# TensorE operands placed modulo 128 bytes in SBUF, and kv weights in rows of 256 columns

## The chip, the cores and the metric

The kernel runs on one core of one Trainium2 chip. The metric is the device time of one execution in microseconds (us). A core has a matrix engine (TensorE, shown as PE, with its weight loads shown apart as PEld), VectorE (DVE), ScalarE (ACT), GpSimd (POOL) and SyncE (SP), which issues most DMA transfers. Operands of TensorE lie in SBUF, products land in PSUM.

A product on TensorE takes two operands from SBUF. The *stationary* operand (the weights, here always up to 128 columns) is brought in by a weight load; the *moving* operand, of 64 to 512 columns here, is then streamed past it. While one moving operand is streamed, the weight load of the next product is already under way, so two reads of SBUF run side by side. This text calls the *place* of an operand the byte address of its first column within a partition, modulo 128. All columns are 4 bytes.

## The reference

One layer of an encoder is computed for 1024 prompt rows and 64 sample rows of width 1024 (with 512 cached rows behind the sample). Cut to what matters:

```python
z = x @ w_in                       # q, k, v of two kinds of attention, u and v of a gate
o = concat(fox_attention, u * (W_s v + b), stick_breaking_attention)
x = layer_norm(ALPHA * x + rms(o) * g_mix @ w_out)
x = layer_norm(ALPHA * x + relu(x @ w_up) ** 2 @ w_down)     # 1024 -> 4096 -> 1024
```

All products are exact to about float32: each operand is split into a high part and a rest, and three products (high by high, high by rest, rest by high: `PASSES`) are summed. The two products of the MLP are done with seven block products instead of eight (a scheme of Strassen's kind).

## The kernel before

The work runs in four stages, by the times at which TensorE does them.

- *Projections and attention, 0 to 542 us.* `tok_mm` (L476, matmuls at L485) makes k and v of a pair of heads, and the gate's u and v: the stationary operand is a block of 128 rows of x (`xT`, 128 columns), the moving one is 256 columns of a weight tile `wkv` (262 columns for the first pair, which takes the forget gate's 6 columns along). `wkv` holds, for each of 8 blocks of rows, the high part and the rest, each in a row of 262 columns, of which all pairs but the first use 256. `q_stage` (L616, L626) makes q with the weights (`wq`) stationary and 256, 320 or 384 columns of `xT` moving. `qk_rows` (L684), `Unit.b_steps` (L732 to L745) and `Sample` (L822 to L868) are the attention.
- *Mix, 542 to 657 us.* `mix` (L344, L368) multiplies a block of rows of the heads' outputs (`oTb`, stationary) with 512 columns of the output weights, which lie where `xT` was.
- *Up, 657 to 1002 us.* `Chain.product` (L1417, L1429) takes weights (`wa`, `ws`, for the first block `w0_` tiles and `oTb`) as the stationary operand and a column slice of x (`xo`) as the moving one: 288 columns of the tile `xo0` for slice 0, 256 columns of the tiles `xo1` for slice 1. A run has 12 matmuls, four blocks by three passes; runs of slice 0 and slice 1 alternate.
- *Down, 1002 to 1353 us.* `Down.product` (L1884, L1894) takes hidden blocks (`h4a`, `h4b`, or parts of the tiles `wd0_`) as the stationary operand and 512 columns of the down weights as the moving one. Weights for chunk c lie in `wset[c % 2]`: the tiles `wd0_` for even c and `wd1_` for odd c. `sample` (L1931, L1938 and L1940) is the same for the sample rows, with `hs` stationary and `wd` or `b12` moving. The down weights are prepared beside this: `wd_load` reads them by DMA (L1543), `wd_split` and `wd_sums` make high parts and rests and the sums of blocks (ACT L1367; POOL or DVE L215 and L1561), and `h_load` and `h_split` (L1578, L1588 to L1593) do the same for the hidden blocks.

Tiles come from pools on the left and right side of SBUF (`sp`, `sa`, `xpool`, `rp`, `lp`, `dp`, `big`), each of which lays its tiles one behind the other; a tile's place therefore depends on the sizes of the tiles ahead of it. A tile that is given a tag shares one place with the others of that tag. The order of the instructions on each engine is written out in tables of numbers (`ORDER`, L49 to L162) for the first two and a half stages and stands in the code for the rest.

The places of the operands in the program as built, stationary and moving, are these; the last column counts the matmuls of a kind.

| stage, line, columns | stationary | moving | matmuls |
|---|---|---|---|
| kv, u, v L485, 256 | `xT` 64 | `wkv` 16 places, 8 apart | 1472 |
| kv first pair L485, 262 | `xT` 64 | `wkv` 16 places, 8 apart | 208 |
| q L626, 256 to 384 | `wq` 0 | `xT` 64 | 576 |
| attention L684, L742 to L745, 256 | 64 | 64 | 768 |
| mix L368, 512 | `oTb` 0 | weights 64 | 416 |
| up slice 0 L1429, 288 | 96 (672), 64 (588), 0 (84) | `xo0` 96 | 1344 |
| up slice 1 L1429, 256 | 96 (672), 64 (588), 0 (84) | `xo1` 64 | 1344 |
| down L1894, 512 | 64, or 32 for `h4b` | 64 even c, 32 odd c | 1344 |

Of the down products, 672 have equal places and 672 have places 32 apart (552 with the stationary at 64 and the moving at 32, 120 the other way round). Of the 128 sample products (L1938, L1940) 48 have unequal places.

Of the kernel before, what the change touches and what calls it, by code (L numbers as in the profile page):

```python
# [173 lines left out]
def _build(nc, tc, a, es):  # L174
# [64 lines left out]
        nc.sync.dma_start(out.bitcast(F32), in_.bitcast(F32))  # L239


    env = {}
    os_, ys, yrow = {}, {}, {}
    wo = []
# [162 lines left out]
    with ExitStack() as p1:  # L407
# [208 lines left out]
        def q_stage(st, u):  # L616
            j, wq, scale = st["nm"], st["wq"], st["scale"]
            acc = ps.tile([P, 512], F32, name=f"q{j}_{u}", tag="acc", bufs=2)
            last = u == 3
            seq = []  # L620
            for k in range(KT):
                full = (k, 0, u * 256, 384 if last else 256)
                rest = [(k, 1, u * 256, 320 if last else 256), (k, 0, LO + u * 256, 256)]
                seq += [full] + rest if k == 0 else rest + [full]
            for i, (k, hw, c, w) in enumerate(seq):
                nc.tensor.matmul(acc[:, 0:w], wq[:, k, hw, :], xT[k // 4][:, k % 4, c:c + w],  # L626
                                 start=(i == 0), stop=(i == len(seq) - 1))
                if (i + 1) % 8 == 0 and i + 1 < len(seq):
                    yield 0.109 * 8
                    flush()  # L630
            qd = sa.tile([P, 2, 2, 256], F32R, name=f"qd{j}_{u}", tag="qd", bufs=2)
            for h in range(2):
                r = slice(h * DH, (h + 1) * DH)
                nc.scalar.activation(qd[r, h, 0, :], acc[r, 0:256], AF.Copy, scale=scale)
                nc.vector.scalar_tensor_tensor(qd[r, h, 1, :], acc[r, 0:256], scale, qd[r, h, 0, :].bitcast(F32),
                                               op0=ALU.mult, op1=ALU.subtract)
                dma_r(qd[(1 - h) * DH:(2 - h) * DH, h, :, :], qd[r, h, :, :])
            if last:
                qs = sa.tile([P, TS], F32, name=f"qs{j}", tag="kvs", bufs=2)
                nc.scalar.activation(qs, acc[:, 320:384], AF.Copy, scale=scale)  # L640
                nc.vector.scalar_tensor_tensor(qs, acc[:, 256:320], scale, qs, op0=ALU.mult, op1=ALU.add)
                for h in range(2):
                    r = slice(h * DH, (h + 1) * DH)
                    for s in (h, 1 - h):
                        ss = slice(s * DH, (s + 1) * DH)
                        nc.scalar.activation(qsz[ss, h, 0, r], qs[r], AF.Copy)
                        lo_sub(nc.gpsimd, qsz[ss, h, 1, r], qs[r], qsz[r, h, 0, r])
            st["qd"][u] = qd
            yield 0.109 * 8
# [242 lines left out]
            return r[0:TS]  # L892

        def sgu_load(col, nm):
            w = sp.tile([P, KT, 2, 262], F32R, name=nm, tag="wkv", bufs=1)
            load_w(w, 0, col, P)
            load_w(w, P, col + P, P)
            return w
# [111 lines left out]

        def load_kv(st):
            dve = (1,) if st["quick"] else ()
            w = st["wkv"] = sp.tile([P, KT, 2, 262], F32R, name=f"wkv{st['nm']}", tag="wkv", bufs=1)
            if st["first"]:

                gates = []
# [19 lines left out]
        def kv_all(j, us=range(5)):  # L1036
            st = pairs[j]
            nm = st["nm"]
            for u in us:
                if u == 4:  # L1040
                    if st["first"]:
                        forget(0)
                    yield from slots("kn", 1, 1)
                    st["kn"] = sa.tile([P, 2, TS], F32R, name=f"kn{nm}", tag="kn", bufs=1)
                    st["vn"] = sa.tile([P, 1, 2, P], F32R, name=f"vn{nm}", tag="vn", bufs=1)
                    yield from kv_stage(st, [NB], st["kn"], st["vn"])
                    continue
                yield from slots("kp", 1, 8)
                kt = sa.tile([P, 2, 256], F32R, name=f"kp{nm}_{u}", tag="kp", bufs=10)
                vt = sa.tile([P, 2, 2, P], F32R, name=f"vp{nm}_{u}", tag="vp", bufs=10)  # L1050
                st["kp"].append(kt)
                st["vp"].append(vt)
                yield from kv_stage(st, [2 * u, 2 * u + 1], kt, vt)
# [14 lines left out]
        def fill():  # L1068
# [19 lines left out]
            yield from slots_free()  # L1088
            yield from sgu_u(wu)
            preps(2, sa)  # L1090
            env["oTb"] = sp.tile([P, 2, KT, 2, P], F32R, name="oTb", tag="wkv", bufs=1)
            for t in range(MIXED):
                while not ready(t):
                    yield None
# [184 lines left out]

    xst = ExitStack()  # L1280
    xpool = xst.enter_context(tc.tile_pool(name="xpool", bufs=1, side="right", reuse_waits="tile"))
    xo0 = xpool.tile([P, 7, 4, 2, NS[0]], F32R, name="xo0")
    xo1 = []
    p3 = ExitStack()
    rp = p3.enter_context(tc.tile_pool(name="rp", bufs=1, side="right", reuse_waits="tile"))
# [210 lines left out]
            back.append(x_samp())  # L1496

    n1 = 4 * 2 * NS[1]
    xw = [big.tile([P, q * n1], F32R, name=f"xo1{q}", tag="xw") for q in (4, 3)]
    xo1 += [x.rearrange("p (o k h c) -> p o k h c", o=q, k=4, h=2) for x, q in zip(xw, (4, 3))]  # L1500
    prep0_b(raws0, 1 - ORD.index(ORD[-1]) % 2)
    x2, x3 = x_pair(2), x_pair(3)
# [339 lines left out]
    with ExitStack() as p3:  # L1842
# [105 lines left out]
        def norm(t):  # L1948
            if t not in lst:

                lst[t] = ident[:, 16 * t:16 * t + 16] if t < NB else dp.tile([P, 16], F32, name="lstb")
            return lst[t]

        def moments(t, half, n=P):
# [330 lines left out]
```

## Time and profile before

| | us |
|---|---|
| median of 3 runs | 1366.65 (1365.5 to 1367.38) |
| span of the profiled execution | 1364.0 |
| TensorE busy | 1311.0 |
| VectorE busy | 997.4 |
| ScalarE busy | 720.4 |
| GpSimd busy | 623.1 |

The profiled execution's own time is its span, 1364.0 us from the first to the last instruction; the median of the runs is 2.65 us longer, which holds what lies around the span and the spread of the runs.

A row of the costliest groups names the line, the engine, the operation, the tile written and the tiles read, the shape and the count, then the busy time and the mean duration of one in ns. That duration runs from the start of a matmul to its modelled end, so it holds the length of TensorE's pipeline and overlaps the next matmul's. What counts for the time is the distance from one start to the next, called the *spacing* here. The chain of work that ended last shows it directly: a piece "x24" with its time is 24 starts. The timeline shows merged runs with the time from the first start to the last end, so that the spacing is that time less the duration of one, shared by one matmul fewer than the run has, or the distance to the next row's start.

### The profile page before, as it was taken

To read this page: it belongs to the slowest core of one execution; us is meant where nothing else is said; L and a number is where in the kernel's file an instruction comes from. 1 tells how busy PE (TensorE), PEld (TensorE's weight loads), DVE (VectorE), ACT (ScalarE), POOL (GpSimd) and SP (SyncE) were. 2 spreads that over 40 slices of the span, in tenths; PEclk is the share of its full clock that TensorE was granted. 3 is DMA by queue.
4 is the path that set the end of the run, shared out by engine and by line. 5 is a ranking of instruction groups with operands and counts; after the bars stand their busy time and mean duration, and the time that the engine had idled before them with its cause. 6 is when DMAs were issued, how large, how long until landed. Compare 5 with 4: busy or idle time off the path is not lost.

```text
span 1364.0 us, 24318 instructions
## 1 busy us (share of the span) xinstructions
PE 1311.0 (96%) x8827; PEld 1195.2 (88%) x8827; DVE 997.4 (73%) x1797; ACT 720.4 (53%) x1561; POOL 623.1 (46%) x666
## 2 busy tenths in 40 slices
PE   7999999999989998999999999999999999999996
PEld 7999989999988997777899999999987787887774
DVE  4577666576888389778876877877687676767777
ACT  4366566576656376344532322322267676767665
POOL 3222222255675457757402321221176665655557
PEclk9999999999999999999999999999999999999999
DMA  7445564131403257432253435334568344434333
GB/s 227 111 121 150 163 205 127 55 96 44 104 17 83 60 183 255 138 116 78 70 174 119 144 120 172 133 131 157 180 226 280 124 146 144 143 120 158 102 138 131
DMA packets 158048, 185.64 MB, mean 136 GB/s; under 512 B 27740, under 2 KB 116124, under 8 KB 157928
## 3 DMA queue, kind: packets, MB, share of 16 engines
q1 hardware_dynamic: 155832, 183.01, 42.1%
q8 instruction: 70, 1.15, 0.3%
q10 hardware_dynamic: 2096, 1.07, 0.3%
q14 instruction: 50, 0.41, 0.1%
HBM read 117.65 MB, written 60.10 MB: 130 GB/s over the span
## 4 chain that ended last, share of the span: by engine, by line
PE 58%; DVE 12%; DMA 10%; POOL 8%; ACT 6%; issue 5%; SPq 0%; ACTq 0%; DVEq 0%; POOLq 0%
PE zA L1429 9%; PE mx L368 6%; PE zD L1429 6%; PE kvsb L485 5%; PE A L1894 5%; PE kvfox L485 3%; PE zB L1429 3%; PE zC L1429 3%; POOL wd L215 3%; PE D L1894 2%; DMA rd<-w_down 2%; DMA raw<-w_in 2%; POOL rd L1561 2%; DMA awa<-h_dr 2%; DVE snsb L668 2%
## 5 line engine op out<-in xcount | busy, mean ns | idle before, releaser
L215 POOL TENSOR_TENSOR wa<-wr,wa 128x512 fp32r<-128x512 f32 x41 | 65.0, 1612 | 219.2 <-ACT wa L1367 219.2
L215 POOL TENSOR_TENSOR wd<-rd,wd 128x512 fp32r<-128x512 f32 x77 | 101.3, 1326 | 109.0 <-ACT wd L1367 103.8
L368 PE MATMUL mx<-xT,oTb 128*128 128x512 f32 (+1 forms) x416 | 103.9, 401 | 1.4 <-DVE oTb L215 1.3
L1429 PE MATMUL zD<-xo,ws 128*128 128x288 f32 (+1 forms) x720 | 97.3, 289 | 0.4 <-DVE hh L1443 0.4
L1429 PE MATMUL zA<-xo,ws 128*128 128x288 f32 (+1 forms) x720 | 97.0, 289 | 0.0
L1429 PEld LDWEIGHTS zD<-xo,ws 128*128 128x128 f32 x720 | 93.5, 189 | 0.7 <-DVE hh L1443 0.7
L1429 PEld LDWEIGHTS zA<-xo,ws 128*128 128x128 f32 x720 | 93.4, 189 | 0.0
L368 PEld LDWEIGHTS mx<-xT,oTb 128*128 128x128 f32 (+1 forms) x416 | 75.3, 186 | 20.2 <-DVE oTb L215 2.1
L485 PE MATMUL kvfox<-wkvfox,xT 128*128 128x256 f32 (+3 forms) x624 | 89.1, 290 | 3.5 <-ACT wkvfox L461 3.0
L1561 POOL TENSOR_TENSOR rd<-rd 128x512 f32<-128x512 f32 x56 | 79.3, 1417 | 24.1 <-DVE b L215 21.8
L485 PE MATMUL kvsb<-wkvsb,xT 128*128 128x256 f32 (+1 forms) x624 | 88.6, 287 | 0.3 <-ACT wkvsb L461 0.3
L1367 ACT ACTIVATE wd<-rd 128x512 fp32r<-128x512 f32 x105 | 63.6, 624 | 45.1 <-POOL rd L1561 23.3
L1894 PE MATMUL A<-wd,wd 128*128 128x512 f32 x312 | 84.3, 399 | 2.0 <-DVE acc L1861 1.7
L670 POOL TENSOR_TENSOR sgsb<-sgsb,snsb 128x127 f32<-128x127 f32 (+7 forms) x48 | 59.6, 1244 | 57.5 <-DVE snsb L668 48.3
L485 PEld LDWEIGHTS kvfox<-wkvfox,xT 128*128 128x128 f32 (+1 forms) x624 | 80.1, 189 | 5.5 <-ACT wkvfox L461 3.4
L485 PEld LDWEIGHTS kvsb<-wkvsb,xT 128*128 128x128 f32 (+1 forms) x624 | 79.4, 187 | 0.7 <-ACT wkvsb L461 0.5
L668 DVE TENSOR_TENSOR_SCAN snsb<-snsb,one 128x128 f32<-128x128 f32 (+7 forms) x48 | 71.8, 1499 | 10.7 <-ACT snsb L667 9.8
L1440 ACT ACTIVATE sn<-zA 128x256 f32<-128x256 f32 (+1 forms) x80 | 31.0, 390 | 83.8 <-PE zA L1429 70.0
L1894 PEld LDWEIGHTS A<-wd,wd 128*128 128x128 f32 x312 | 58.8, 190 | 18.5 <-DVE acc L1861 3.3
L1894 PE MATMUL A<-wd,h4a 128*128 128x512 f32 x240 | 64.6, 394 | 1.2 <-POOL wd L215 0.7
L1650 ACT ACTIVATE ws<-wr 128x1024 fp32r<-128x1024 f32 x28 | 29.1, 1057 | 59.4 <-DVE wr L1379 59.4
L1894 PEld LDWEIGHTS A<-wd,h4a 128*128 128x128 f32 x240 | 44.8, 188 | 12.2 <-POOL wd L215 1.1
(551 smaller groups left out, 3746.8 us busy)
## 6 DMA issues: line engine op xcount, KB each, us to landing
h_dr<-hh SPq DMA_DIRECT2D x30, 512.0 KB, 3.2
rd<-w_down SPq DMA_DIRECT2D x30, 512.0 KB, 4.4
wr<-w_up SPq DMA_DIRECT2D x13, 1024.0 KB, 5.5
hr<-h_dr SPq DMA_DIRECT2D x31, 384.0 KB, 4.4
h_dr<-hh SPq DMA_DIRECT2D x30, 384.0 KB, 3.4
raw<-w_in SPq DMA_DIRECT2D x44, 256.0 KB, 3.4
wo_dr<-swo SPq DMA_DIRECT2D x32, 256.0 KB, 2.3
xT<-wo_dr SPq DMA_DIRECT2D x8, 1024.0 KB, 7.9
```

The lines of the kernel that those rows point to most:

```text
L215: eng.tensor_tensor(out, src, hi.bitcast(F32), op=ALU.subtract)
L368: nc.tensor.matmul(acc[0:m], oT[:, k, hx, 0:m], wo[k // 4][hw][:, k % 4, cs], start=(i == 0), stop=(i == len(seq) - 1))
L485: nc.tensor.matmul(acc[0:n, c0:c0 + n1 - n0], xT[k // 4][:, k % 4, c:c + n], wt[:, k, hw, n0:n1], start=(i == 0), stop=(i == len(seq) - 1))
L668: nc.vector.tensor_tensor_scan(g[:, 0:n][:, ::-1], g[:, 0:n][:, ::-1], one.broadcast_to([P, n]), 1.0, op0=ALU.mult, op1=ALU.bypass)
L670: nc.gpsimd.tensor_tensor(s[:, 0:n - 1], s[:, 0:n - 1], g[:, 1:n], op=ALU.mult)
L1367: nc.scalar.activation(hi, raw, AF.Copy)
L1429: nc.tensor.matmul(z, w[:, hw, k], xop(s, bo, hx)[:, k, :], start=(new and k == 0 and j == 0), stop=(k == 3 and j == 2), skip_group_check= ...
L1440: nc.scalar.activation(c, z, AF.Copy)
L1561: eng.tensor_tensor(r[:, o], r[:, x], r[:, y], op=ALU.subtract)
L1650: nc.scalar.activation(ws[:, 0, q, c], src[:, q], AF.Copy)
L1894: nc.tensor.matmul(z, h[:, hx, q, o], wset[self.c % 2][q][:, hw, wb], start=((n in (0, 3) or n == 1 and self.c == 0) and q == 0 and j == 0 ...
```

## The change

The order of the instructions on every engine, and what each waits for, stay as they are; no instruction is added or removed. Only places change, and the stride of one tile. A helper `pad` takes a small unused tile out of a pool so that what follows lies further on. Rows of `wkv` become 256 columns wide for all but the first pair (and for the gate's weights), so that all their places are equal. `oTb` and the `xo1` tiles start 16 columns (64 bytes) into tiles that are longer by as much. The last tile on the right, `lstb`, becomes 40 columns wide, which shifts the tiles ahead of it.

```diff
+    def pad(pool, n):
+        n_pad.append(pool.tile([P, n // 4], F32, name=f"pad{len(n_pad)}", tag=f"pad{len(n_pad)}"))
+    n_pad = []
...
             qd = sa.tile([P, 2, 2, 256], F32R, name=f"qd{j}_{u}", tag="qd", bufs=2)
+            if st["first"] and u == 0:
+                pad(sa, 64)
...
         def sgu_load(col, nm):
-            w = sp.tile([P, KT, 2, 262], F32R, name=nm, tag="wkv", bufs=1)
+            w = sp.tile([P, KT, 2, 256], F32R, name=nm, tag="wkv", bufs=1)
...
-            w = st["wkv"] = sp.tile([P, KT, 2, 262], F32R, name=f"wkv{st['nm']}", tag="wkv", bufs=1)
+            w = st["wkv"] = sp.tile([P, KT, 2, st["nv"]], F32R, name=f"wkv{st['nm']}", tag="wkv", bufs=1)
...
                 kt = sa.tile([P, 2, 256], F32R, name=f"kp{nm}_{u}", tag="kp", bufs=10)
+                if st["first"] and u == 0:
+                    pad(sa, 64)
...
-            env["oTb"] = sp.tile([P, 2, KT, 2, P], F32R, name="oTb", tag="wkv", bufs=1)
+            env["oTb"] = sp.tile([P, 16 + 4 * KT * P], F32R, name="oTb", tag="wkv", bufs=1)[:, 16:].rearrange(
+                "p (a k h c) -> p a k h c", a=2, k=KT, h=2)
...
+    pad(xpool, 64)
     xo0 = xpool.tile([P, 7, 4, 2, NS[0]], F32R, name="xo0")
+    pad(xpool, 96)
...
-    xw = [big.tile([P, q * n1], F32R, name=f"xo1{q}", tag="xw") for q in (4, 3)]
+    xw = [big.tile([P, 16 + q * n1], F32R, name=f"xo1{q}", tag="xw")[:, 16:] for q in (4, 3)]
...
-                lst[t] = ident[:, 16 * t:16 * t + 16] if t < NB else dp.tile([P, 16], F32, name="lstb")
+                lst[t] = ident[:, 16 * t:16 * t + 16] if t < NB else dp.tile([P, 40], F32, name="lstb")
```

The places in the changed program as built:

| stage, columns | stationary | moving | apart before | apart now |
|---|---|---|---|---|
| kv, u, v, 256 | 64 | 0 | 0 to 64 in steps of 8 | 64 |
| kv first pair, 262 | 64 | 16 places | 0 to 64 in steps of 8 | the same |
| q, 256 to 384 | 0 | 64 | 64 | 64 |
| attention, 256 | 0 | 64 | 0 | 64 |
| mix, 512 | 64 | 64 | 64 | 0 |
| up slice 0, 288 | 64 (1308), 0 (36) | 0 | 0, 32 | 64 (1308), 0 (36) |
| up slice 1, 256 | 64 (1308), 0 (36) | 0 | 0, 32, 64 (84) | 64 (1308), 0 (36) |
| down and its sample products, 512 | 64 | 64 | 0, 32 | 0 |

## The prediction

> **What bounds the kernel now.** I read first the page's engines, then the shares of the chain of waits over the whole span, then that chain stage by stage, and last single runs of matmuls.
>
> ```profile
> span 1364.0 us, 24318 instructions
> PE 1311.0 (96%) x8827; PEld 1195.2 (88%) x8827; DVE 997.4 (73%) x1797; ACT 720.4 (53%) x1561; POOL 623.1 (46%) x666
> ...
> PE 58%; DVE 12%; DMA 10%; POOL 8%; ACT 6%; issue 5%; SPq 0%; ACTq 0%; DVEq 0%; POOLq 0%
> ```
>
> TensorE is busy almost throughout, yet only 58% of the chain lies on it. So a matmul that gets faster helps the end only where the chain runs over it. By line:
>
> ```profile
> by line: PE zA L1429 9.1%; PE mx L368 6.4%; PE zD L1429 6.1%; PE kvsb L485 4.8%; issue 4.7%; PE A L1894 4.6%; PE kvfox L485 3.2%; PE zB L1429 3.1%; PE zC L1429 3.0%; POOL wd L215 2.9%; PE D L1894 2.4%; DMA rd<-w_down 2.1%; DMA raw<-w_in 1.7
> ```
>
> The up stage (zA to zD) holds 21.3% of the chain, 290 us; mix holds 6.4%, 87 us; kv holds 8.0%, 109 us. For the down stage I took its chain in two stretches, 1022 to 1157 us and from 1157 us to the end:
>
> ```profile
> by line: PE A L1894 47.0%; PE D L1894 23.8%; PE B L1894 11.3%; PE ds L1940 5.2%; PE ds L1938 5.1%; issue 2.7%; DVE acc L1859 2.3%; DVE wd L215 0.6%; DVE acc L1861 0.6%; ACT h4a L1588 0.5%; ACT st L1592 0.5%; DVE h4b L1593 0.4%; DVE h4a L159
> ```
>
> ```profile
> by line: DMA rd<-w_down 13.8%; POOL wd L215 13.1%; POOL rd L1561 10.7%; issue 9.6%; DMA awa<-h_dr 7.7%; ACT wd L1367 5.1%; ACT st L1592 4.4%; ACT wd L1588 2.7%; DVE acc L2006 2.4%; POOL awa L1996 2.3%; POOL awa L1992 2.3%; DVE wd L215 2.0%;
> ```
>
> Up to 1157 us the chain is TensorE's. Behind that it runs for 207 us over the preparation of down weights and hidden blocks (DMA, POOL, ACT) and the closing norm, with no matmul in it, although TensorE is busy without a break there too:
>
> ```profile
> 1100.00:1200.00 100.00, 100.00 (x435) 80.12 (x435) 74.21 (x115) 67.54 (x135) 57.96 (x46) 1.00 0.44 147
> ```
>
> ```profile
> PE A L1894 <- POOL wd L215: 0.7, 1, 0.7
> ```
>
> The second row is TensorE's first wait after that, around 1302 us: it had just used up its lead over the preparation. Both run at one pace, and a faster TensorE will wait here.
>
> **What a matmul costs by its places.** The change adds and removes no instruction and moves none in any queue, SP's and POOL's included; what is to be costed is the spacing of matmuls whose places change. The trace of before already has several distances. 512 columns, places equal (the first down products, timeline) and places 32 and 64 apart (down with chunk 1's weights, and mix; the chain's pieces):
>
> ```profile
> 1005.06 2.88 PE L1894 MATMUL B<-wd,h4a 128*128 128x512 f32 x12
> 1007.78 2.88 PE L1894 MATMUL A<-wd,h4a 128*128 128x512 f32 x12
> 1010.50 2.88 PE L1894 MATMUL D<-wd,h4a 128*128 128x512 f32 x12
> ```
>
> ```profile
> 1074.15 2.80 PE A L1894 x12
> ...
> 613.47 2.80 PE mx L368 x12
> ```
>
> Equal: 12 matmuls from 1007.78 to 1010.50, 226.7 ns each. Unequal: 2.80/12 = 233.3 ns. The difference of 6.6 ns is one of place: same line, same shape, same clock.
>
> 256 columns, 64 apart, occurs in the first block of slice 1 (stationary in `oTb`, timeline), and in q; 256 at other distances in kv and in the up stage:
>
> ```profile
> 678.01 1.52 PE L1429 MATMUL zD<-xo,oTb 128*128 128x256 f32 x12
> 679.37 1.68 PE L1429 MATMUL zA<-xo,oTb 128*128 128x256 f32 x12
> ...
> 45.67 5.90 PE L626 MATMUL qfox<-xT,wqfox 128*128 128x256 f32 x48
> ```
>
> ```profile
> 458.89 4.41 PE kvsb L485 x37
> 64.07 3.30 PE qfox L626 x23
> ```
>
> 64 apart gives two spacings: (679.37 - 678.01)/12 = 113.3 ns in the first, but in q (5.90 - 0.29)/47 = 119.4 ns, a slow start of the run included, some 118 ns without it. A run keeps the one it falls into. kv, at mixed distances, has 4.41/37 = 119.2 ns. The last row is q's run of 384, 320 and 256 columns in turn, all 64 apart: 143.5 ns for 320 columns on average, 0.448 ns a column, against 113.3/256 = 226.7/512 = 0.443 at the short ones. For the up stage, runs of 12 by form and one whole pair of runs:
>
> ```profile
> L1429 PE MATMUL zA<-xo,ws 128*128 128x288 f32 x360 | 53.1, 297 | 0.0
> L1429 PE MATMUL zA<-xo,ws 128*128 128x256 f32 x360 | 47.5, 281 | 0.0
> ```
>
> ```profile
> 732.85 3.04 PE zA L1429 x24
> ```
>
> 53.1 us in 30 runs is 1.770 us a run; less the last one's 0.297, over 11, is 133.9 ns for 288 columns. The same way 118.4 ns for 256. Together 252.3 ns, and the pair of runs has 3.04/12 = 253.3 ns.
>
> **The sum.** Each term is matmuls on the chain times what one saves.
>
> *Mix, 64 apart to equal.* 87 us at 233.3 ns are 374 matmuls, by 6.6 ns: 2.5 us. The value is measured; as bounds I keep 2 to 2.5.
>
> *Down, 32 apart to equal.* 71 to 82% of 135 us up to 1157 us are 475 matmuls; those of chunks 1 and 3 and the products whose hidden blocks lie at 32 make about 60%, 285, by 6.6 ns: 1.9 us. The 377 unequal ones behind 1157 us save 2.5 us of TensorE's time, which I cost at nothing: the preparation covers it, and is late next. Bounds 0.9 to 4.4.
>
> *Up, slice 1, 256 columns to 64 apart.* 290/0.2533 = 1146 pairs on the chain. One of 256 saves 5.1 ns at the short spacing (118.4 to 113.3) and 0.4 at the long one (118). Nothing in the trace tells which of them a run falls into that follows a run of 288, so I take the middle, 2.8 ns: 3.2 us. Bounds 0.5 to 5.8.
>
> *Up, slice 0, 288 columns to 64 apart.* No row has this width at this distance. The upper bound is the short spacing's 0.443 ns a column, 127.6 ns, a saving of 6.3 ns or 7.2 us. The lower: no saving; or, if 288 cost what the mean of 320 does, 143.5 ns, a loss of 9.6 ns or 11 us, which nothing in the rows excludes at this very width. The nearest row is that of q's mixed run at the same distance, 0.448 ns a column: 129.1 ns, a saving of 4.8 ns and 5.5 us. I take it. The 36 + 36 matmuls with equal places now, 84 + 84 of which some were 64 apart before, move 0.2 us and are left out.
>
> *kv, u, v, 256 columns to 64 apart.* 8.0% of the chain is 109 us; some 25 us of that is the first pair with 262 columns, which stays as it is. 84 us at 119.2 ns are 705 matmuls. They are cut up by attention, so I take the middle of the two again, 115.7 ns: 3.5 ns, 2.5 us. Bounds 0.8 to 4.2.
>
> *Attention, 256 columns, equal to 64 apart.* 768 matmuls, half of them on the chain by the stage's share, by 2.5 ns: 1.0 us; bounds 0 to 2.
>
> *Rows of 256 instead of 262 for ACT, POOL and DVE.* The split of kv weights writes rows that are shifted by 24 bytes from one to the next; that of the q weights does not:
>
> ```profile
> L461 ACT ACTIVATE wkvsb<-raw 128x512 fp32r<-128x512 f32 x12 | 7.3, 624 | 5.0 <-DMA raw<-w_in 4.7 <-PE kvsb L485 0.4
> L461 ACT ACTIVATE wqsb<-raw 128x512 fp32r<-128x512 f32 x6 | 3.6, 624 | 2.1 <-PE qsb L626 1.7 <-PE qfox L626 0.4
> ```
>
> Both take 624 ns: no term. The unused tiles cost no time, since nothing touches them.
>
> Together 2.5 + 1.9 + 3.2 + 5.5 + 2.5 + 1.0 = 16.6 us. In the first stage the chain leaves TensorE often:
>
> ```profile
> by line: PE kvsb L485 12.1%; PE kvfox L485 8.2%; issue 6.7%; DMA raw<-w_in 4.3%; DVE snsb L668 3.9%; PE qsb L626 3.6%; DMA rwo<-w_out 3.6%; PE qfox L626 3.3%; PE Sfox L684 3.0%; PE ptfox L732 2.5%; PE Ssb L684 2.4%; PE ptsb L732 2.1%; PE sg
> ```
>
> Other paths (DVE's scan L668, DMA) lie close behind there, and the preparation of down weights is nearly late before 1157 us already. I take 2 us off for both, an estimate from the two terms they threaten (3.5 and 1.9). That leaves 14.6 us: the profiled execution would come to 1349.4, and with the 2.65 us by which the median of the runs lies over the span, 1352.
>
> **A rule that speaks against it.** The rows say that a weight load slows the moving read by place, 226.7 against 233.3 ns. The Trainium skill, "SBUF — State Buffer", section "Who interferes with whom", says that PE and ACT never wait on anyone, and its table of paths gives TensorE's weight loads a second, independent read port. By that rule places would be without effect, the sum would be 0 and the time 1366.65. The trace does not bear it out for 512 columns; for the other widths it stays a rival.
>
> **The rivals.**
>
> *All of it at the short spacing.* Up saves 5.8 + 7.2, kv 4.2, attention 2, mix and down 4.4: 23.6 us, 1343. For it: the first block's slice 1 stayed at 113.3 ns through all its products. Against: q's run of 48 at 118.
>
> *Only the 512s gain.* If 64 apart is worth nothing in the up stage and in kv, 4.4 + 0.5 + 0.8 = 5.7 us, less some of the down term: 1362. For it: q's 118 ns.
>
> *It doesn't do what it says.* The spacing belongs to something that goes along with the place, such as which tile is read, or what is gained is waited for elsewhere: 1366.65. For it: the chain's 42% off TensorE. Against: 2.80/12 = 233.3 both in mix and in down, for quite different tiles.
>
> *Slower: 288 columns dislike 64 apart.* With 143.5 ns a matmul the up stage loses 11 us, and if the 256s then have 118 ns, the rest gains 5.7: 1372. It decides from 5.7/1146 = 5 ns on, at 139 ns. For it: nothing but that the row is missing. Against: 256, 320 and 384 columns, on both sides of 288, do well at this distance.
>
> TensorE's clock is no rival, though a wait can cost it: where TensorE had waited before 1023 us, its clock fell,
>
> ```profile
> 1023.00:1027.00 4.00, 3.78 (x10) 0.57 0.92 340
> ```
>
> ten matmuls in 4 us instead of some 17, about 1.7 us. New waits behind 1157 us may bring such stretches, but off the chain.
>
> **How the numbers follow.** The forecast's own case, 1347 to 1357, gets 0.44; all short 0.21; only the 512s 0.19; no effect 0.09; slower 0.07. About 0.2%, 2.7 us, is what a measurement of this kernel can tell from no change. The first three all lie beyond it: faster 0.84, same 0.09, slower 0.07. The range of 1341 to 1363 holds those three and leaves out the last two, with the bounds of the costs inside it.
>
> **What would show it.** After the change mix and every down product should have 226.7 ns; mix's run of 12 in the chain 2.72 us instead of 2.80. The up stage's pair of runs should fall from 3.04 us to some 2.93 (129.1 + 115.6 ns); at 2.89 all is short, at 3.02 nothing is, above 3.11 the fourth rival is true. A run of 37 in kv should take 4.2 to 4.3 us. New waits of TensorE on POOL or ACT should stand between 1140 and 1300 us. I am wrong if the up stage's pair doesn't move, since it holds over half of the sum, or if the preparation of down weights takes back what mix and up gained.

## The result

The changed kernel takes 1359.67 us (median of 8 runs, 1356.17 to 1361.91), the kernel before, run beside it, 1366.08 us (8 runs, 1362.63 to 1368.37): a ratio of 0.9954, with a 95% interval of 0.9939 to 0.9969, so 6.3 us faster (4.2 to 8.3). The direction was right and the time lies inside the range; the gain is less than half of the 14.6 us forecast. A second comparison of the two gave 0.9955 (0.9941 to 0.9969).

The profiled execution of the changed kernel has a span of 1358.4 us, 5.6 less than before. Its page, engines and the shares of the chain that ended last:

```profile
span 1358.4 us, 24318 instructions
PE 1305.0 (96%) x8827; PEld 1190.8 (88%) x8827; DVE 998.3 (73%) x1797; ACT 719.3 (53%) x1561; POOL 620.6 (46%) x666
...
PE 71%; DVE 12%; DMA 6%; POOL 4%; ACT 4%; issue 3%; SPq 1%; ACTq 0%; DVEq 0%; POOLq 0%
```

TensorE is busy 6.0 us less, each other engine within 2.5 us of before. TensorE's share of the chain went up from 58 to 71%, where the share of a TensorE that is faster and waited for elsewhere should have gone down. The chain from 1157 to 1340 us says where:

```profile
by line: PE A L1906 43.6%; PE D L1906 21.0%; PE B L1906 10.5%; PE ds L1952 4.0%; PE ds L1950 4.0%; POOL awa L2008 2.6%; DVE wd L1605 1.3%; POOL acc L2008 1.3%; POOL acc L2004 1.3%; POOL awa L2004 1.3%; DVE acc L1916 1.0%; issue 0.9%; PE las
```

Before, this stretch held no matmul; now it is TensorE's. (All of after's lines lie 5 to 12 further on.) The pieces of the chain that the prediction named, and the up stage's runs by form:

```profile
615.37 2.79 PE mx L373 x12
...
706.98 3.00 PE zA L1441 x24
709.98 3.00 PE zB L1441 x24
712.98 2.94 PE zA L1441 x24
```

```profile
460.56 4.36 PE kvsb L490 x37
```

```profile
L1441 PE MATMUL zA<-xo,ws 128*128 128x288 f32 x360 | 52.6, 295 | 0.0
L1441 PE MATMUL zA<-xo,ws 128*128 128x256 f32 x360 | 46.6, 279 | 0.0
```

Mix has 2.79/12 = 232.5 ns a matmul where 226.7 was forecast: almost nothing. The up stage's pair of runs has 2.94 or 3.00 us, not 2.93 throughout. By the prediction's way of reckoning, 52.6/30 less 0.295, over 11, is 132.6 ns for 288 columns (133.9 before), and the same for 256 is 115.8 ns (118.4 before). Kv's run went from 4.41 to 4.36 us, 117.8 ns.

So mix, kv and the 288 columns gained less than forecast. In the text below the *distance* is the place of the stationary operand less that of the moving one, modulo 256 bytes unless said otherwise. The places of after, modulo 256, are these, with the mean distance from one start to the next, taken over all matmuls of a kind with the waits left out:

| matmuls | distance | ns before | ns after |
|---|---|---|---|
| mix, 512 | 64, then 128 | 233.2 | 232.3 |
| down, 512, half of them | 0, then 0 | 228.2 | 228.4 |
| down, 512, the other half | 32 or 224, then 128 | 233.2 | 232.8 |
| up, 288 | many, then 64 or 192 | 133 to 136 | 132.6, 132.9 |
| up, 256, distance 64 | 0 or 32, then 64 | 118.8, 118.2 | 115.5 |
| up, 256, distance 192 | the same, then 192 | 118.8, 118.2 | 116.1 |
| kv, 256 | 16 places, then 192 | about 119 | 117.7 |
| attention, 256 | 0, then 64 | 119.1 | 116.7 |

Equal modulo 128 turned out to be 128 apart modulo 256 for mix and half of down, and "64 apart" to be 64 for some and 192 for others.

### The profile page after: what moved, and what is told of

It is laid out like the page before. It is cut to its first block, busy times and chain, and to the rows that moved or that the text cites. A ratio compares the mean times of both kernels' runs of the same rounds, so it can differ in the third digit from the quotient of the medians.

```text
span 1358.4 us, 24318 instructions
## 1 busy us (share of the span) xinstructions
PE 1305.0 (96%) x8827; PEld 1190.8 (88%) x8827; DVE 998.3 (73%) x1797; ACT 719.3 (53%) x1561; POOL 620.6 (46%) x666
## 4 chain that ended last, share of the span: by engine, by line
PE 71%; DVE 12%; DMA 6%; POOL 4%; ACT 4%; issue 3%; SPq 1%; ACTq 0%; DVEq 0%; POOLq 0%
PE A L1906 10%; PE zA L1441 9%; PE mx L373 6%; PE zD L1441 6%; PE D L1906 5%; PE kvsb L490 5%; PE kvfox L490 3%; PE zB L1441 3%; PE zC L1441 3%; PE B L1906 2%; DMA rwo<-w_out 2%; PE qsb L631 2%; PE Sfox L691 1%; PE qfox L631 1%; DVE snsb L675 1%
## 5 line engine op out<-in xcount | busy, mean ns | idle before, releaser
L1873 DVE TENSOR_TENSOR acc<-acc,A 128x512 f32<-128x512 f32 x73 | 49.1, 679 | 10.9 <-PE A L1906 10.9
```

The costliest lines, as they stand in the source:

```text
L1873: nc.vector.tensor_tensor(out, out if other is None else other, bank, op=ALU.add)
```

## The experiments

**Matmuls alone, by distance.** A kernel that does nothing but runs of 36 matmuls, each run at one distance, with a short matmul `k` between runs:

```diff
+        def run(nm, n, d, triples, k0=0):
+            # d: stationary less moving place, in bytes
...
+            for k in range(triples):
+                s = [st[:, d // 4 + 256 * (2 * ((k0 + k) % 4) + h):][:, 0:P] for h in range(2)]
+                m = [mv[:, 1024 * (2 * ((k0 + k) % 4) + h):][:, 0:n] for h in range(2)]
+                for j, (hx, hw) in enumerate(((0, 0), (0, 1), (1, 0))):
+                    nc.tensor.matmul(acc[:, 0:n], s[hw], m[hx], ...)
```

> This kernel leaves the whole encoder out and writes only a piece of one output; it runs nothing but runs of 36 matmuls of 512, 288 and 256 columns, each run with one distance in bytes between the places of its stationary and its moving operand (0, 32, 64 ... 480, and 16, 512, 576, 640, 704, 768, 896, 960). Distance is counted modulo 1024 throughout. Theory A (the spacing goes by the distance modulo 256): 512 columns have some 227 ns at distances 0, 256, 512 and 768 alone, 232 to 233 ns at 128, 384, 640 and 896 as well as at 64; 288 columns have some 133 ns at 64 and show at some other distance what the best place would be. Theory B (modulo 128, as the change has it; what mix shows after the change is due to something else in that stage): 227 ns at 128, 384, 640 and 896 too. Theory C (modulo 512): 227 ns at 0 and 512 only, 232 ns at 256 and 768. For 256 columns 113 ns, 118 ns or both at the same distance are expected; if the three runs of one distance differ, the spacing is not fixed by the distance alone.

Its timeline, 512 columns at distances 0 (`za`), 64 (`zc`), 128 (`ze`), 192 (`zg`) and 256 (`zi`):

```profile
30.41 8.43 PE L35 MATMUL za<-mv,st 128*128 128x512 f32 x36
...
64.07 8.59 PE L35 MATMUL zc<-mv,st 128*128 128x512 f32 x36
...
98.12 8.60 PE L35 MATMUL ze<-mv,st 128*128 128x512 f32 x36
...
132.17 8.44 PE L35 MATMUL zg<-mv,st 128*128 128x512 f32 x36
...
165.88 8.42 PE L35 MATMUL zi<-mv,st 128*128 128x512 f32 x36
```

A run of 36 is 0.17 us longer at 64 and at 128 than at 0 and at 256. The means between starts, by distance modulo 256 (distances that differ by 256 or 512 agreed within 1.2 ns for 512 and 288 columns):

| columns | 0 | 16 | 32 | 64 | 96 | 128 | 160 | 192 | 224 |
|---|---|---|---|---|---|---|---|---|---|
| 512 | 227.3 | 226.7 | 233.2 | 233.3 | 234.2 | 233.0 | 233.4 | 229.0 | 233.3 |
| 288 | 131.7 | 132.0 | 133.3 | 133.3 | 133.2 | 133.3 | 131.6 | 131.9 | 133.4 |
| 256 | 119.7 | 118.3 | 118.3 | 113.6 or 117.8 | 117.3 or 118.7 | 118.6 to 120.0 | 119.8 | 117.8 | 116.8 or 117.8 |

Theory A holds: for 512 and 288 columns the distance counts modulo 256, not 128 and not 512. Two more readings follow. 288 columns have the 129.1 ns of the forecast at none of these distances; at 64 they are among the slow ones. And 256 columns have the short spacing at 64 alone of these, in some runs and not in others; at 192 never in this kernel. (Within the encoder the up stage's 192s had 116.1 ns on average, so some of their runs are short there; no run here shows why.)

```profile
813.63 4.35 PE L35 MATMUL zc<-mv,st 128*128 128x256 f32 x36
...
817.85 4.33 PE L35 MATMUL zc<-mv,st 128*128 128x256 f32 x36
...
822.07 4.46 PE L35 MATMUL zc<-mv,st 128*128 128x256 f32 x36
```

These are three runs of the same matmuls at distance 64: two short, one long. With no other engine at work there, the Trainium skill's rule in "SBUF — State Buffer", section "Who interferes with whom", that weight loads have a read port of their own, doesn't carry over to time: TensorE's two reads cost each other up to 7 ns here.

**All 512s equal modulo 256.** On top of the change, `oTb` and the right-hand buffers of down are moved by 128 bytes more:

```diff
-            env["oTb"] = sp.tile([P, 16 + 4 * KT * P], ...)[:, 16:].rearrange(
+            env["oTb"] = sp.tile([P, 48 + 4 * KT * P], ...)[:, 48:].rearrange(
...
-    lst[t] = ... dp.tile([P, 40], F32, name="lstb")
+    lst[t] = ... dp.tile([P, 72], F32, name="lstb")
```

> The changed kernel with two places moved: mixing's stationary tile by 128 bytes more and down's right-hand buffers by 128 bytes more, so that all products of 512 columns have equal places modulo 256. Theory A (modulo 256, and TensorE's time counts to the end): mix falls from 232 to 227 ns, 374 x 5 = 1.9 us on the chain, and the 717 down products that were 128 apart from some 232 to 227, 3.6 us; together 5.5 us, about 1354. Theory B (the preparation of down weights is the limit behind 1157 us, as the prediction had it): only mix's 1.9 us and some 1.5 us of the first half of down, about 1356.5. Theory C (modulo 128 was right, or equal modulo 512 is needed): mix stays at 232 ns; about 1358 to 1360.

Measured 1357.42 us against 1364.4 before: 0.9949 (0.9936 to 0.9961), 7.0 us. To compare it with the change on one chip, it was run again beside the changed kernel:

> The kernel with all 512-column products equal modulo 256, once more, beside the changed kernel. Its profile had 228.4 ns in mix and 227.2 in down where the changed kernel's had 232.3 and 232.8 in half of down. Theory A (TensorE's time counts to the end): 5 us below the changed kernel. Theory B (down's preparation covers what lies behind 1157 us): 1.5 to 3 us below it. Theory C (neither stage's matmuls are what the end waits for): no difference.

> The changed kernel once more, beside the next two, so that all three stand against the same runs of the kernel before: 5.5 to 7.5 us faster than before if the first comparison was right.

1357.56 against 1358.19 us; ratios to the kernel before 0.9951 (0.9933 to 0.9970) and 0.9955 (0.9941 to 0.9969). The matmuls did what theory A said: 228.4 ns in mix, 227.2 in all of down, 391 x 3.9 + 717 x 5.6 = 5.5 us of TensorE's time. Of these about 0.6 us is to be seen in the two medians, less than their uncertainty: theory B or C. The chain from 1157 to 1340 us of this kernel:

```profile
by line: POOL wd L215 14.3%; DMA rd<-w_down 12.3%; POOL rd L1573 12.0%; issue 10.6%; DMA awa<-h_dr 8.4%; ACT wd L1379 5.5%; ACT st L1604 4.3%; DVE acc L1873 3.1%; POOL awa L2008 2.6%; DVE h4a L1605 2.4%; ACT wd L1600 2.3%; DVE wd L1605 1.9%
```

With the last 5.6 ns gone from half of down's matmuls, the chain is off TensorE again. But which path the chain names there says little of what down's matmuls cost. The first row is the kernel with kv's rows alone (below), whose down has the places of before; the second is the kernel before with nothing but the 512s made equal (next experiment):

```profile
by line: PE A L1894 44.8%; PE D L1894 21.0%; PE B L1894 10.6%; PE ds L1940 4.2%; PE ds L1938 4.0%; POOL awa L1996 2.6%; DVE wd L1593 1.3%; POOL acc L1996 1.3%; POOL acc L1992 1.3%; POOL awa L1992 1.3%; DVE acc L1904 1.0%; PE lastB L1894 0.9
by line: PE A L1895 30.4%; PE D L1895 13.4%; PE B L1895 6.8%; DMA awa<-h_dr 5.1%; POOL wd L215 4.2%; DMA rd<-w_down 3.7%; issue 3.5%; POOL rd L1562 3.4%; ACT st L1593 3.2%; PE ds L1941 3.1%; PE ds L1939 3.0%; POOL awa L1997 2.6%; ACT wd L15
```

TensorE has 85% of the stretch in a kernel whose down is that of before, where it had none, and 57% with all 512s short. TensorE's path and the preparation's are nearly equally long there, and small differences decide which of them the chain follows.

**The same places, nothing else changed.** The two edits above on the kernel before:

> The kernel before with all products of 512 columns at equal places modulo 256, and nothing else: 391 matmuls of mix and 609 and some of down go from 233 to 227 or 228 ns, up, kv, q and attention keep their places. Theory A (all of it counts): 391 x 5 + 660 x 6 = 5.9 us faster than before. Theory B (only mix and the first half of down count): 2 + 1.9 = 3.9 us. Theory C (nothing of down counts): 2 us.

1363.56 against 1365.07 us, 0.9991 (0.9977 to 1.0005): 1.2 us (-0.7 to 3.1). Theories A (5.9) and B (3.9) are out; what there is fits mix alone (2), and also nothing at all.

**How far the preparation of down lies behind TensorE.** 112 matmuls of the second half cut short:

```diff
+                        m = 128 if self.c >= 4 and q == 0 and j == 1 else 512
-                        nc.tensor.matmul(z, h[:, hx, q, o], wset[self.c % 2][q][:, hw, wb],
+                        nc.tensor.matmul(z[:, 0:m], h[:, hx, q, o], wset[self.c % 2][q][:, hw, wb][:, 0:m],
```

> The changed kernel with 112 matmuls of the second half of down (chunks 4 to 7, one of the six of each product) cut from 512 to 128 columns, so a part of the low-order products is left out there. TensorE has 112 x some 165 ns = 18 us less to do behind 1190 us. Theory A (TensorE is what the end waits for): some 18 us faster than the changed kernel, 1341. Theory B (the preparation of down weights and hidden blocks runs at TensorE's own pace, as the prediction said of the stretch behind 1157 us): TensorE waits instead; at most 3 us faster, 1356 or above. Between the two the time says how far the preparation lies behind TensorE.

1358.07 against 1365.14 us, 0.9945 (0.9933 to 0.9958): 7.5 us (5.7 to 9.1), 1.2 more than the changed kernel's 6.3, less than either interval's half. The 18 us of the expectation were too many. By the starts in the trace a cut matmul takes 59 ns instead of some 231, but the one behind it takes 284: together 119 ns less, 13 us for the 112. Theory A asks for these 13 us, and they didn't come. TensorE's waits from 1140 to 1360 us, the three longest of this kernel and then the only one of the changed kernel (engine and line, what it waited for, us in total, times, longest):

```profile
PE A L1907 <- DVE acc L1873: 3.5, 4, 1.8
PE B L1907 <- ACT B L1894: 1.0, 1, 1.0
PE A L1907 <- POOL wd L215: 0.8, 2, 0.5
```

```profile
PE A L1906 <- DVE acc L1873: 1.0, 1, 1.0
```

TensorE now waits 7.5 us in all in this stretch, where it waited 1.0 us in the changed kernel. Behind 1157 us the preparation runs within a few us of TensorE's own pace, as the prediction had it, and most of what TensorE saves there is lost in waits.

**Kv rows alone**, on the kernel before (`wkv` in rows of 256 columns, so at distance 192):

```diff
-            w = sp.tile([P, KT, 2, 262], F32R, name=nm, tag="wkv", bufs=1)
+            w = sp.tile([P, KT, 2, 256], F32R, name=nm, tag="wkv", bufs=1)
...
-            w = st["wkv"] = sp.tile([P, KT, 2, 262], ...)
+            w = st["wkv"] = sp.tile([P, KT, 2, st["nv"]], ...)
```

> The kernel before with the rows of 256 columns in kv weights alone (products of kv, u and v 64 apart, all else at its old places). Theory A (64 apart gives kv the long spacing, some 117.7 ns against 119): 705 x 1.3 = 0.9 us faster, about 1365.2. Theory B (kv falls into the short spacing when it is done alone, 113.3): 4 us faster, 1362. Theory C (the spacing of kv is not what its stage waits for): 1366, no difference.

1364.59 against 1364.4 us: 0.9999 (0.9989 to 1.0009), so 0.1 us (-1.2 to 1.5). Kv's matmuls had 117.6 ns: 63 of its 74 runs lay at 118, 4 at 113. Theory B is out; between A's 0.9 us and C's nothing the time can't tell.

**The up stage's places alone**, on the kernel before (the two pads in `xpool` and the 16 columns ahead of the `xo1` tiles, nothing else):

```diff
+    pad(xpool, 64)
     xo0 = xpool.tile([P, 7, 4, 2, NS[0]], F32R, name="xo0")
+    pad(xpool, 96)
...
-    xw = [big.tile([P, q * n1], F32R, name=f"xo1{q}", tag="xw") for q in (4, 3)]
+    xw = [big.tile([P, 16 + q * n1], F32R, name=f"xo1{q}", tag="xw")[:, 16:] for q in (4, 3)]
```

> The kernel before with the up stage's places alone changed (288 and 256 columns 64 apart; mix, down, kv and attention at their old places). Theory A (the sum by the spacings measured after the change): 1146 pairs x (0.9 + 2.8) ns = 4.2 us faster, about 1361.9, two thirds of what the whole change gave. Theory B (the prediction's 288 columns at 129.1 ns): 8.7 us, 1357.4. Theory C (the gain of the change is not in the up stage): within 1.5 us of the kernel before.

1361.18 against 1364.4 us: 0.9977 (0.9969 to 0.9986), 3.1 us (1.9 to 4.2). That is nearest to theory A, whose 4.2 us lie at the end of the interval. It is the largest of the pieces of the change that were run by themselves. The length of the stages in the profiles, from the first start in a stage to the first in the next (down: to its last start), says the same:

| kernel | mix, us | up, us | down, us |
|---|---|---|---|
| before | 115.8 | 344.3 | 350.8 |
| kv alone | 116.3 | 344.2 | 348.2 |
| 512s alone | 114.2 | 344.7 | 347.0 |
| up alone | 115.6 | 341.5 | 351.1 |
| after (two profiles) | 116.2, 117.4 | 339.6, 341.2 | 348.1, 348.4 |
| after with equal 512s (two) | 114.6, 114.7 | 340.4, 340.4 | 346.6, 346.6 |

The up stage follows its places: 344.2 to 344.7 without the change, 339.6 to 341.5 with it. Down's length goes from 346.6 to 351.1 us with little regard to them: kv alone and up alone have the places of before in down, and 348.2 and 351.1 us. One profile stands for each figure, so differences of a us or two are not to be read.

**What picks the short spacing: width, place, or the moment.** Matmuls alone again, with the moving place varied at a fixed distance, the width varied, and 19 widths of the one matmul ahead of a run:

```diff
+        def run(nm, n, d, triples, at=0):
+            # at: the moving place
...
+                s = [st[:, (at + d) // 4 + 256 * (2 * (k % 4) + h):][:, 0:P] for h in range(2)]
+                m = [mv[:, at // 4 + 1024 * (2 * (k % 4) + h):][:, 0:n] for h in range(2)]
...
+        for n in range(32, 260, 12):
+            for r in range(3):
+                shake("s", n)
+                run("s", 256, 64, 12)
```

> Again nothing but runs of 36 matmuls, the encoder's work left out. It asks three things. First, is it the distance or the place: with both operands moved by 32, 64, 96, 128 and 192 bytes at the same distance, Theory A (distance modulo 256) gives 512 columns 227 ns at distance 0 and 233 ns at 64 in all five places, and 256 columns 113 or 118 ns; Theory B (the place itself) gives values that change from place to place. Second, how the spacing at distance 64 goes with the width: if 288 columns lose because they are no multiple of 256, the short 0.443 ns a column (106.3 ns at 240, 113.3 at 256, 170 at 384) is met at 256 and perhaps 384 and 512 columns alone, and the widths between lie 4 to 6 ns above it; if the spacing simply rises with the width, all widths from 240 to 448 lie on one line. Third, what picks 113 or 118 ns for 256 columns at distance 64: if the moment at which a run begins does, the spacing follows the width of the one matmul ahead of it (32 to 248 columns, three runs of each), the same in all three; if it is chance, the three differ. Distances of 36 to 92 show how wide the band of the short spacing is: a few bytes, or some 48 to 80.

512 columns had 226.7 to 227.8 ns at distance 0 and 233.3 to 233.4 at 64, in all five places: for them the distance decides. At distance 64 the spacing per column goes up and down with the width: 0.443 to 0.445 or 0.460 ns at 256, 0.455 to 0.459 at 264, 0.454 at 272, 0.463 at 288, 0.458 at 320, 0.455 at 352, 0.451 at 448 (0.446 at distance 192). That is neither a line nor a threshold: each width has its own good distances. Among the distances from 36 to 92, 256 columns had 113.3 to 114.3 ns at 52 and 76 and 117.7 to 120.1 at 36, 44, 60, 68, 84 and 92. And 256 columns at 64 had 113.3 to 113.9 ns in all three runs behind matmuls of 68, 80, 92, 104, 212 and 248 columns, 117.8 in all three behind 164, and behind the other twelve widths both, in turn from run to run. So it isn't chance, and it isn't set by the places either: the one matmul ahead of a run, and for most widths what came before it, decide. That this works through the moment at which the run begins is the likely reading; no run varies the moment by itself.

This kernel also had 113.3 to 114 ns for 256 columns at distance 168 in all three runs. That was tried in the encoder.

**The up stage at 168**, on the kernel with equal 512s:

```diff
-    pad(xpool, 96)
+    pad(xpool, 224)
...
-    xw = [big.tile([P, 16 + q * n1], ...)[:, 16:] for q in (4, 3)]
+    xw = [big.tile([P, 22 + q * n1], ...)[:, 22:] for q in (4, 3)]
```

> All 512-column products equal modulo 256, and the up stage's products of 256 columns 168 bytes apart (modulo 256) instead of 64 and 192. Alone on TensorE that distance gave 113.3 to 114 ns in all three runs, where 64 gave 113 or 118 and 192 gave 118. Theory A (the table of distances holds inside the kernel): zA to zD of 256 columns fall from 116 to 113.5 ns, 1146 x 2.5 = 2.9 us below the kernel with equal 512s, about 1354.6. Theory B (behind a run of 288 columns a run of 12 falls into either spacing whatever the distance): 116 ns stay, 1357.5.

**Kv, u, v and q at 168 as well** (`wkv` starts 6 columns into its tile, `wq` 26):

```diff
+        def w256(nm):
+            return sp.tile([P, 6 + 512 * KT], F32R, name=nm, tag="wkv", bufs=1)[:, 6:].rearrange(
+                "p (k h c) -> p k h c", k=KT, h=2)
```

> The same, and kv, u, v and q with 256 columns 168 apart as well. Theory A (spacings hold, and TensorE's time counts in the first stage): kv from 117.7 to 113.5, 705 x 4.2 = 3.0 us, q 0.4 us: 3.4 us below the one before, about 1351. Theory B (the first stage waits for other paths, as its chain and the run with kv alone suggest): kv's spacing falls just as far but the time stays at that of the one before. Theory C (the table does not hold for kv's runs, which attention cuts up): 117 to 118 ns stay.

Both theories of the first fell: 1364.07 and 1364.58 us against 1365.14, ratios 0.9991 (0.9979 to 1.0003) and 0.9992 (0.9975 to 1.0010). The gain of the change was gone. The up stage's runs of the first:

```profile
L1441 PE MATMUL zA<-xo,ws 128*128 128x288 f32 x360 | 53.0, 296 | 0.0
L1441 PE MATMUL zA<-xo,ws 128*128 128x256 f32 x360 | 48.1, 283 | 0.0
```

(48.1/30 - 0.283)/11 is 120.0 ns; all but one of its 107 runs lie at 120, and kv's lie there too (119.8). The up stage took 347.9 us. Against the kernel with equal 512s the 256s went from 116.2 to 120.0 ns and the 288s from 132.7 to 133.6, 4.7 ns a pair, which over 1146 pairs is 5.4 us; the two ratios to the kernel before, 0.9951 and 0.9991, lie 5.5 us apart. So here the up stage's spacings count nearly in full at the end. Here the distance was the same as in the matmuls alone, but not the places: stationary at 40 and moving at 128 there, stationary at 192 and moving at 24 here.

**Both places**, matmuls alone:

```diff
+        for w, b in (("a", 0), ("b", 24), ("c", 32), ("d", 64)):
+            for i in range(32):
+                for r in range(3):
+                    run("u" + w + AB[i], 288, 8 * i, 0, 4)
+                    run("z" + w + AB[i], 256, 8 * i, b, 4)
```

(`run` takes the stationary and the moving place now.)

> Matmuls alone once more, the encoder's work left out, now with both places varied in steps of 8 bytes. First as in the up stage: 12 of 288 and 12 of 256 columns in turn with the same stationary operand, its place from 0 to 248 modulo 256, the 256s' moving operand at 0, 24, 32 and 64, the planes of the 288s 1152 bytes apart as in the kernel. Then as in kv: runs of 24 of 256 columns, the stationary at three places and the moving one from 0 to 248. Theory A (the distance alone decides): rows with the same distance agree whatever the moving place, 113.5 ns at 168 among them; then what the kernel with 168 showed, 120 ns in every run, has to come from the company of the 288s, and the rows in turn show 120 at 168 too. Theory B (both places count): at distance 168 a moving operand at 24 gives 120 ns and one at 0, 32 or 64 gives 113.5. Theory C (it is the other work in the kernel, not the places): 113.5 everywhere at 168.

Its timeline, runs of 12 of 256 columns, `zav` with the moving operand at 128 and `zby` with it at 152, both at distance 168; `zai` at 128 and distance 64:

```profile
222.07 1.53 PE L35 MATMUL zav<-mv,st 128*128 128x256 f32 x12
...
539.62 1.60 PE L35 MATMUL zby<-mv,st 128*128 128x256 f32 x12
...
104.92 1.53 PE L35 MATMUL zai<-mv,st 128*128 128x256 f32 x12
```

113.3 ns in the first and the last, 119.8 in the second: theory B in its first half. With the moving operand at 152, an odd multiple of 8, all 32 distances had 119.3 to 122.0 ns and nothing helped. Theory B's other half, 113.3 at the other aligned places, failed at 160, where distance 168 had 120.0. In the runs of 24, two stationary places 64 bytes apart, 128 and 192, gave the same spacing at the same distance, within 0.6 ns at all 32 distances (130.0 ns, the worst of all, at distance 152 in both). So in these runs the distance modulo 256 decides, together with the place modulo 64. In the runs of 12 that alternate with 288 columns that isn't all: with the moving operand at 192 instead of 128, distance 64 gave 115.2, 117.8 and 117.8 ns and distance 168 gave 120.1, 113.3 and 113.3, where at 128 all six runs had 113.3. Distances 64 and 192 differ too, here for 24 matmuls in a run, three runs each, distance 64 (`kga`) and 192 (`kgq`):

```profile
1737.97 8.32 PE L35 MATMUL kga<-mv,st 128*128 128x256 f32 x72
...
1874.85 8.64 PE L35 MATMUL kgq<-mv,st 128*128 128x256 f32 x72
```

113.3 ns against 117.8. The change has kv at 192.

**All 256s of the up stage at 64, then kv too.** Equal 512s, all stationary operands of the up stage at 192 and `xo1` at 128 (48 columns in place of 22 in the edit above); in the second kernel `wkv` starts 32 columns into its tile, `wq` as before.

> The kernel with all 512s equal modulo 256, and in the up stage every stationary operand at the same place modulo 256, the 256s' moving operand at 128, so that all products of 256 columns are 64 apart and none 192; both places are multiples of 64. Matmuls alone gave 113.3 ns for such pairs of runs (245.6 with the 288s). Theory A (place and distance decide, 64 and 192 are not the same): the 256s' mean falls from 116 to between 113.3 and 115.4, 1146 x 0.7 to 2.7 = 0.8 to 3.1 us below the 1357.5 of equal 512s, about 1355.5. Theory B (in the kernel a run falls into either spacing at both distances): 116 stays, 1357.5.

> The same with kv, u and v at 64 instead of 192. Matmuls alone gave 113.4 ns at 64 and 117.8 at 192 for runs of 24. Theory A (the spacing holds, and counts in the first stage): kv from 117.6 to 113.5 or 114, 705 x 4 = 2.8 us below up64. Theory B (the first stage waits for other paths): kv has 113.5 to 114 ns, and the start of mix and the time are up64's within 1 us. Theory C (the short spacing is not met in kv's cut-up runs): 117 ns.

The first took 1357.92 us, 0.9953 (0.9933 to 0.9972); the up stage's 256s had 115.5 ns, and of their 107 runs 58 lay at 113 or 114 and 48 at 118. Its time can't tell the theories apart, since the 288s lost what the 256s gained: with equal 512s alone a pair has 116.2 + 132.7 = 248.9 ns, here 115.5 + 133.3 = 248.8. A place that gives 113.3 ns with TensorE alone gives both spacings within the encoder, so neither theory holds quite. The second took 1355.62 us against 1364.14, 0.9940 (0.9923 to 0.9958), 8.2 us (5.7 to 10.5); kv had 116.0 ns (117.6 at distance 192), 705 x 1.6 = 1.1 us, and its profile starts mix 3.4 us earlier than up64's, which is more than that explains; one profile stands for each. Its ratio is the lowest of all, but its interval overlaps with that of the change and of up64: that it beats the change is likely and not shown, and whether kv's spacing counts stays open.

## Why the prediction was right or wrong

- *Mix, 2.5 us: wrong, 0.3 by its spacing.* The step that failed is "64 apart to equal": the rows of equal places, "MATMUL B<-wd,h4a" at 1005 us, were equal modulo 256 as well, and the prediction took what they showed for equality modulo 128. At 128 apart a matmul has 232.3 ns, (233.2 - 232.3) x 374 = 0.3 us. Equal modulo 256 gave 228.4.
- *Down, 1.9 us: wrong, 0.1*, by the same step: the half that should have gained went from 233.2 to 232.8 ns. That nothing behind 1157 us would count was right: about 13 us less of TensorE's work brought 1.2 us, with new waits. The sign named for it, new waits between 1140 and 1300 us in the changed kernel, didn't come, since the matmuls there had not become faster: TensorE waited 1.0 us behind 1140 us, where it had waited 2.6 before. It came with the cut matmuls (7.5 us); with equal 512s there were 2.2 us of waits, no more than before.
- *Up, slice 1, 3.2 us: right.* By the runs' rows (118.4 - 115.8) x 1146 = 3.0 us. The middle of the two spacings was taken for want of a row, so that its size came out is luck, though the runs do divide between the two. Part of these matmuls lie at 192 and not at the 64 that the term is about.
- *Up, slice 0, 5.5 us: wrong, 1.5.* (133.9 - 132.6) x 1146. The step that failed is the 129.1 ns, taken from q's mixed run. The mean of 384, 320 and 256 columns says nothing of 288: alone at that distance 320 columns have 146.6 ns, not the 143.5 of that mean, and 288 have 133.3. This term was the greatest and the worst sized.
- *Kv, 2.5 us: the spacing wrong, the time not seen.* At 192 the runs lie at the long spacing: 119 to 117.7 ns, 0.9 us by that; the run with kv alone gave 0.1 (-1.2 to 1.5). The step that failed is "the middle of the two again": 64 and 192 were taken as one distance.
- *Attention, 1.0 us: the spacing right,* 119.1 to 116.7 ns where 2.5 ns were forecast; its time wasn't measured by itself.
- *Rows of 256 for ACT, POOL and DVE, nothing: right,* as far as their busy times show: ACT 720.4 and 719.3 us, DVE 997.4 and 998.3, POOL 623.1 and 620.6.

With the measured spacings the same sum is 0.3 + 0.1 + 3.0 + 1.5 + 0.9 + 0.9 = 6.7 us, against 6.3 (4.2 to 8.3) measured. Four of the spacings did not hold. That the counts of matmuls on the chain did is borne out by the whole, but not piece by piece: the up stage alone gave 3.1 us (1.9 to 4.2) where its spacings give 4.5. The pieces run by themselves (up 3.1, kv 0.1) leave 3.1 us for mix, down and attention, where the spacings give 1.3. Nor is there a sign of the 2 us that the forecast took off for other paths. So the agreement of 6.7 with 6.3 is in part luck, and how the gain divides outside the up stage stays open.

Of the rivals, "all short" and "288 columns dislike 64 apart" are refuted by 132.6 ns. "Only the 512s gain" came out the other way round: the 512s alone gained nothing clear of noise (1.2 us, -0.7 to 3.1) and the up stage most. "It doesn't do what it says" was true of mix, of half of down and of kv, in a way that it hadn't named: the places were what the change says, but the modulus was another.

## What to carry to other kernels

Before a rule on addresses is taken from a trace, write down each case with the full address, not with the remainder that the change itself uses: here every "equal" case of before agreed modulo 256 too, and one look at that would have put mix and down at nothing. A spacing that has two values at one place is no figure for a run in other company: measure the shape itself, alone, and then once more within the kernel. And when the chain runs over one engine for long, cut that engine's work there and see whether the end moves; a chain that names TensorE for 83% of a stretch (the rows A, D, B and ds) was within a few us of another path.

## What the runs showed of the hardware

That the spacing of a matmul goes with the places of its two operands could be read from the first profile (226.7 and 233.3 ns for 512 columns); the kernels of matmuls alone show it with no other engine at work, and show how fine the pattern is. The spacing depends on the distance of stationary and moving operand modulo 256 bytes (512 columns: 227 to 234 ns, 3%) and, for 256 columns, on the place as well, in runs of 24 modulo 64 (113.3 to 130.0 ns, 15%). A moving operand of 256 columns at 152 had 119.3 ns or more at every distance. At some distances there are two stable spacings (113.3 and 117.8 ns for 256 columns at 64), and a run keeps the one that it begins with, which the width of the one matmul ahead of it can change.
